# MLP of a two-layer diffusion step: the residual's tiles pass one by one to the up matrix's rings, and the down matrix's first piece gets a buffer of its own

## The chip, the cores and the metric

The kernel runs on one core of a Trainium2 chip. The metric is the device time of one launch in microseconds (us); lower is better. PE is the matmul engine (TensorE), DVE, ACT and POOL are VectorE, ScalarE and GpSimd, SP is the engine that issues most DMA transfers.

## The reference, cut to what matters

One inference step of a two-layer backbone: layer 0 mixes tokens with an RG-LRU, layer 1 with latent attention, and each layer ends in an MLP with a squared ReLU. All of it is fp32. There are 1024 latent tokens and 128 context tokens, of width 1024; the hidden width is 4096.

```python
def sq_relu_mlp(h, w1, w2):
    a = jax.nn.relu(h @ w1)
    return (a * a) @ w2
...
    for l in range(DEPTH):
        sh1, sc1, g1, sh2, sc2, g2 = adaln_params(c, ada_w[l], ada_b[l])
        h = modulate(rms_norm(xs, norm_mix[l]), sh1, sc1)
        ...  # token mixer -> out
        xs = xs + g1[:, None, :] * out
        h = modulate(rms_norm(xs, norm_mlp[l]), sh2, sc2)
        xs = xs + g2[:, None, :] * sq_relu_mlp(h, mlp_w1[l], mlp_w2[l])
```

## The kernel before, in words

The 1152 tokens stand as columns, in three chunks of 384. The residual `X` is three SBUF tiles `X[c]` of 128 x 8 x 384 fp32 (12 KB in each partition), in a pool `xp`. An fp32 product is made from three matmuls (`mm3`: L148, L151, L152) of a high and a low part of each operand. A weight piece is 128 x 1024: a load on SP's queue gives `raw` (L112), a cast on ACT gives `whi` (L166), a subtraction on DVE or POOL gives `wlo` (L167). The two results go to slots that `wslot` takes in turn from a list of pools, `wcycle`.

`mlp` runs once for each layer, at some 500 to 1290 us and 2040 to 2800 us of the span. Its up matrix takes chunks 0 and 1 with seven products per 2 x 2 block (Strassen-Winograd), and chunk 2 plainly:

- `filler(0, 8)`: the first 8 plain pieces on chunk 2.
- 16 chains `p`, 108 matmuls each. `prep(p + 1, 0..2)`, called at three places within chain `p`, loads two raws (`r`) for the next chain, makes R0 and R1 (splits on POOL in layer 0, on DVE in layer 1), subtracts within the raws (`add`, L459) and splits them again as TY and TX on DVE. Eight hidden results of a chain are squared or summed in tiles `st` and stored to DRAM (`put`, L422: from ACT's queue, or from SP's in `tail`). The pool `upx` holds 8 `st` tiles, 4 `raw` tiles and one `whi`/`wlo` pair (the slot "u" of `wcycle`), in the place of `xp`, which is released before the chains: the residual lies in DRAM (`xs_d`) meanwhile. In layer 0 two jobs `ada` stand in each chain: a load of a row block of the conditioning matrix (L181) and two dot products on DVE (L172).
- `filler(8, 8, bring)`: the last 8 plain pieces on chunk 2, 24 matmuls each. `upx` is released and `xp` allocated anew. After each piece `bring` issues a load of half an X tile (L586, 768 KB) and some loads of hidden halves (`load`, L570, 384 KB, each with a cast on ACT and a subtraction on DVE).

The down matrix follows: `prep_down` makes its pieces V[0], V[1], ... two from each raw. An even V is split from the raw as it came; then four subtractions change the raw (L607) and the odd V is split from it, all of this on POOL. The splits go first to four slots "g" of the pool `gx`, which takes the place of chunk 2's high and low parts (`gpool`). Every third "g" slot first does one `ada` job, in a buffer of `gx` with the tag "ada". The first products use V[0], V[2], then V[1]; each result is added to X by DVE (`residual`, L339).

A scheduler reorders the instructions on each engine, by its own model of times. Only what `keep_in_program_order` marks keeps its place. Tiles of a released pool are taken over one at a time, when the last reader of what lay there is done.

Of the kernel before, what the change touches and what calls it, by code (L numbers as in the profile page):

```python
# [15 lines left out]
D = 1024  # L16
# [4 lines left out]
CH = 384  # L21
NCH = 3
# [43 lines left out]
class Emit:  # L66
    def __init__(self, nc, tc, ins, outs):
        self.nc, self.tc, self.I, self.O = nc, tc, ins, outs
        self.piece_i = 0
        self.opened = []  # L70
        self.pending = []
        self.wpx = None
        self.pin = False
        self.cap = 1 << 30
        self.upx = self.gx = None
        self.on_dve = False
        self.wcycle, self.wi = ["wp"], 0
        self.ready = []
        self.used, self.oldest = set(), 0
        self.ada_i = 0  # L80
        self.ada_jobs = []
        self.ada_quota = 0.0
        self.ada_rate = 0.0
# [31 lines left out]
    def wslot(self):  # L115

        kind = self.wcycle[self.wi % len(self.wcycle)]
        self.wi += 1
        if kind == "g":
            if self.ada_i % 3 == 0:  # L120
                self.ada(1, self.gx)
            self.ada_i += 1
        pool, n = {"wp": (self.wp, 3), "x": (self.wpx, 1), "u": (self.upx, 1), "g": (self.gx, 4)}[kind]
        return tuple(pool.tile([128, 1024], F32R, tag=t, name=t, bufs=n) for t in ("whi", "wlo"))

    def wsplit(self, raw, eng, n=1024):
# [287 lines left out]
    def mlp(self, p0, base, l, H, after_acc, after):  # L414
        nc = self.nc
        hid_d = self.hid_d[l]

        up_row = lambda m: base + (m // 4) * 8 + m % 4
# [29 lines left out]
        filler(0, 8)  # L448
        for c in range(NCH):
            self.need(c)  # L450
        self.release(self.xp)
        self.upx = self.alloc(name="upx", bufs=1, side="right", reuse_waits="tile")
        st = lambda: self.upx.tile([128, CH], F32, tag="st", name="st", bufs=8)
        A11, A12 = (tuple(t[:, 4 * i:4 * i + 4] for t in H[0]) for i in range(2))
        A22 = tuple(t[:, 4:8] for t in H[1])
        C2 = [tuple(t[:, 4 * i:4 * i + 4] for t in H[2]) for i in range(2)]
# [5 lines left out]
        def prep(p, part):  # L462
            if p == 16:
                if part:
                    self.on_dve = True
                    self.cap = p0 + 8 + part
                    self.prefetch(self.cap)
                return
            m = 4 * (p // 2) + p % 2
            if part == 0:  # L470
                r = [self.raw(up_row(i), *((self.upx, 4) if p else ())) for i in (m, m + 2)]
                W[p] = {"r": r, "R0": self.wsplit(r[0], leng)}
                return
            w = W[p]
            r0, r1 = w["r"]
            a, b = slice(0, 512), slice(512, 1024)
            if part == 1:
                w["R1"] = self.wsplit(r1[:, b], leng, 512)
                add(r0[:, a], r1[:, a], r0[:, a], ALU.subtract)
                add(r1[:, a], r1[:, b], r1[:, a], ALU.subtract)  # L480
                add(r1[:, b], r1[:, b], r0[:, a], ALU.subtract)
                add(r0[:, b], r0[:, b], r1[:, b], ALU.subtract)
            else:
                w["TY"] = self.wsplit(r1, nc.vector)
                w["TX"] = self.wsplit(r0, nc.vector)

        self.wcycle, self.wi = ["wp", "wp", "wp", "x", "u"], 0
        for i in range(3):
            prep(0, i)
        tail = None  # L490
        for p in range(16):
            m = 4 * (p // 2) + p % 2
            w = W.pop(p)
            if p == 15:
                self.wcycle, self.wi = ["wp", "wp", "wp", "x"], 0
            A = self.bank()
            self.prod(A, w["R0"], 0, A11, 4, True)
# [1 line left out]
            nc.scalar.copy(out=s1, in_=A)  # L499
            if tail:  # L500
                tail()
            prep(p + 1, 0)
            B = self.bank()
            self.prod(B, w["R0"], 4, A12, 4, True)
# [29 lines left out]
            square(h12)  # L534
            put(m, 0, h12)
            prep(p + 1, 2)

            def tail(m=m, A=A, w=w, h11=h11, h12=h12, h22=h22):
                self.prod(A, w["TX"], 4, A22, 4)
                h21, s, d = st(), st(), st()  # L540
                relu2(h21, A)
                add(s, h21, h22)
                put(m, 4, s, nc.sync)
                add(h21, h11, h21, ALU.subtract)
                put(m, 6, h21, nc.sync)
                add(d, s, h11, ALU.subtract)
                put(m, 3, d, nc.sync)
                e = st()
                add(e, h12, d, ALU.subtract)
                put(m, 7, e, nc.sync)  # L550
# [2 lines left out]
                self.ada(2, pin=True)  # L553
        tail()
        self.cap = p0 + 16
        self.release(self.upx)
        self.xp = self.alloc(name="xp", bufs=3, side="right", reuse_waits="tile")
        self.X = []
        D = {}
        used = [0]  # L560

        def load(upto, pin=False):
            while used[0] < min(upto, 72):
                i = used[0]
                if i % 2 == 0:
                    D["t"] = self.cbig(F32R, "hid")
                t = D["t"]
                o = 4 * (i % 2)
                hi, lo = t[:, o:o + 2], t[:, o + 2:o + 4]
                ld = nc.sync.dma_start(lo.bitcast(F32), hid_d[i // 9][:, i % 9])  # L570
                if pin:
                    self.tc.keep_in_program_order(ld)
                self.split(hi, lo, lo.bitcast(F32))
                D[i] = (hi, lo)
                used[0] += 1

        for c in range(NCH):
            self.X.append(self.xp.tile([128, 8, CH], F32, tag="X", name="X"))
        xh = [(c, i) for c in range(NCH) for i in (0, 4)]

        def bring(i):

            if 2 <= i:
                c, k = xh[i - 2]
                self.tc.keep_in_program_order(
                    nc.sync.dma_start(self.X[c][:, k:k + 4], self.xs_d[l][c, :, k:k + 4])  # L586
                )
            load((2, 4, 5, 6, 7, 8, 9, 9)[i], True)

        filler(8, 8, bring)  # L590
        self.on_dve = False
# [5 lines left out]
        V = []  # L597

        def prep_down(upto):
            while len(V) < min(upto, 64):  # L600
                n = len(V)
                if n % 2 == 0:
                    raw = D["raw"] = self.raw(base + (n // 8) * 8 + 4 + n // 2 % 4)
                else:
                    raw = D["raw"]
                    b11, b21, b12, b22 = (raw[:, i * 256:(i + 1) * 256] for i in range(4))
                    sub = lambda out, x, y: nc.gpsimd.tensor_tensor(out=out, in0=x, in1=y, op=ALU.subtract)  # L607
                    sub(b11, b12, b11)
                    sub(b12, b22, b12)
                    sub(b22, b22, b11)  # L610
                    sub(b21, b21, b22)
                V.append(self.wsplit(raw, nc.gpsimd))

        def add_x(c, m, ps):
            self.residual(c, m, ps, l, 5)
# [2 lines left out]
        for d in range(16):  # L618
            g = d // 2
            a12, a11, ca, s2, s1, cb, s3, s4, a22 = (D[9 * g + i] for i in range(9))  # L620
            ch = []
            for i in range(2):
                n = 2 * d + i
# [951 lines left out]
```

## Time and profile before

| | us |
|---|---|
| median of 3 runs (lowest, highest) | 2833.51 (2833.25, 2837.84) |
| profiled execution | 2835.06 |
| its span, from the first to the last instruction | 2833.2 |
| PE busy | 2656.6 (94%) |
| DVE, ACT, POOL busy | 1951.3, 1385.0, 840.8 |
| mean granted PE clock | 0.974 |

A row of the page's costliest groups has line, engine, operation, output<-inputs, shape and count, then the busy time and the mean in ns, then the idle time of the engine just before, with what ended it. In a timeline each row has start and duration in us; the brackets give the idle time before it and its releaser. A `q` behind an engine's name (SPq, ACTq) is that engine's queue issuing a DMA; the row's duration is that of the issue, not of the transfer.

### The profile page before, as it was taken

What the parts mean: (1) busy time and instruction counts of PE and PEld (TensorE: products, weight loads), DVE (VectorE), ACT (ScalarE), POOL (GpSimd) and SP (SyncE); (2) the same over time, 40 slices, a digit from 0 to 9 for tenths busy, and PEclk for the clock granted to TensorE, in tenths of its full rate; (3) what the DMA queues carried; (4) which work ended last, traced back from release to release, by engine and by line L of the source; (5) the groups of instructions that cost most, each with busy time, mean ns of one, the idle gap of its engine ahead of it and who ended that gap; (6) DMA issues with size and microseconds to landing.
All of it is one profiled execution on the core that took longest, in us unless ns stands there. A gap on an engine that the chain in (4) does not pass through costs nothing. (4 is left out here: it accounts for less than half of the span.)

```text
span 2833.2 us, 40867 instructions
## 1 busy us (share of the span) xinstructions
PE 2656.6 (94%) x15355; PEld 2561.3 (90%) x15355; DVE 1951.3 (69%) x3461; ACT 1385.0 (49%) x2446; POOL 840.8 (30%) x544
## 2 busy tenths in 40 slices
PE   5999999999996899997998999998999999799997
PEld 2878798999996899997987999998999999799997
DVE  7778876788865987779455767761675554477777
ACT  3577843645453232334325878881465544333332
POOL 1000013221214877771341000001300000677774
PEclk9999999999997999999998999999999999899998
DMA  6122244455556443434244111116344445433333
GB/s 255 45 82 82 82 156 139 142 189 185 199 176 235 158 136 112 134 101 158 68 132 141 62 48 62 35 52 220 115 153 138 134 144 194 150 123 113 122 124 107
DMA packets 145718, 368.67 MB, mean 130 GB/s; under 512 B 15472, under 2 KB 77744, under 8 KB 143088
## 3 DMA queue, kind: packets, MB, share of 16 engines
q1 hardware_dynamic: 121712, 331.44, 34.7%
q10 hardware_dynamic: 23040, 31.47, 3.1%
q0 software_dynamic: 768, 3.15, 0.4%
q8 instruction: 121, 1.98, 0.3%
q14 instruction: 77, 0.63, 0.1%
HBM read 268.83 MB, written 94.54 MB: 128 GB/s over the span
## 5 line engine op out<-in xcount | busy, mean ns | idle before, releaser
L167 POOL TENSOR_TENSOR wlo<-raw,whi 128x1024 fp32r<-128x1024 f32 x217 | 526.5, 2436 | 1680.8 <-ACT whi L166 1066.1
L166 ACT CAST whi<-raw 128x1024 fp32r<-128x1024 f32 (+1 forms) x349 | 347.2, 1009 | 637.3 <-POOL raw L607 261.1
L148 PE MATMUL ps<-hhi,whi 128*128 128x384 f32 x1576 | 533.0, 342 | 28.5 <-ACT hhi L324 13.2
L151 PE MATMUL ps<-hlo,whi 128*128 128x384 f32 x1576 | 535.3, 340 | 16.3 <-DVE hlo L325 16.1
L152 PE MATMUL ps<-hhi,wlo 128*128 128x384 f32 x1576 | 530.6, 339 | 1.2 <-DVE wlo L167 1.2
L339 DVE SCALAR_TENSOR_TENSOR X<-ps,mod,X 128x384 f32<-128x384 f32 (+2 forms) x768 | 380.4, 534 | 218.7 <-PE ps L152 186.2
L148 PE MATMUL ps<-hid,whi 128*128 128x384 f32 x1408 | 477.2, 342 | 38.8 <-ACT whi L166 20.5
L151 PE MATMUL ps<-hid,whi 128*128 128x384 f32 x1408 | 477.8, 339 | 0.0
L152 PE MATMUL ps<-hid,wlo 128*128 128x384 f32 x1408 | 463.3, 339 | 2.1 <-POOL wlo L167 2.1
L148 PEld LDWEIGHTS ps<-hhi,whi 128*128 128x128 f32 x1576 | 299.1, 190 | 38.7 <-ACT hhi L324 14.4
L151 PEld LDWEIGHTS ps<-hlo,whi 128*128 128x128 f32 x1576 | 300.0, 190 | 21.1 <-DVE hlo L325 21.0
L148 PEld LDWEIGHTS ps<-hid,whi 128*128 128x128 f32 x1408 | 268.8, 191 | 49.9 <-ACT whi L166 23.4
L152 PEld LDWEIGHTS ps<-hhi,wlo 128*128 128x128 f32 x1576 | 299.3, 190 | 3.5 <-DVE wlo L167 2.6
L152 PEld LDWEIGHTS ps<-hid,wlo 128*128 128x128 f32 x1408 | 267.3, 191 | 3.3 <-POOL wlo L167 3.3
L151 PEld LDWEIGHTS ps<-hid,whi 128*128 128x128 f32 x1408 | 269.4, 191 | 0.0
L167 DVE TENSOR_TENSOR wlo<-raw,whi 128x1024 fp32r<-128x1024 f32 (+1 forms) x132 | 151.6, 1158 | 164.8 <-ACT whi L166 163.8
L167 DVE TENSOR_TENSOR hid<-hid 128x768 fp32r<-128x768 f32 x144 | 204.2, 1440 | 77.0 <-ACT hid L166 77.0
L607 POOL TENSOR_TENSOR raw<-raw 128x256 f32<-128x256 f32 x256 | 244.4, 958 | 17.6
L166 ACT CAST hid<-hid 128x768 fp32r<-128x768 f32 x144 | 117.1, 834 | 138.1 <-DMA hid<-hid 119.1
L1277 DVE TENSOR_REDUCE mx<-ps 128x1 f32<-128x384 f32 (+1 forms) x200 | 108.6, 543 | 76.0 <-PE ps L1276 74.5
L151 PE MATMUL ps<-S,whi 128*128 128x384 f32 x384 | 129.2, 336 | 2.7 <-DVE S L167 2.7
L152 PE MATMUL ps<-S,wlo 128*128 128x384 f32 x384 | 129.0, 336 | 0.0
(213 smaller groups left out, 5190.0 us busy)
## 6 DMA issues: line engine op xcount, KB each, us to landing
raw<-wts SPq DMA_DIRECT2D x221, 512.0 KB, 3.7
hid<-hid SPq DMA_DIRECT2D x144, 384.0 KB, 4.3
raw<-ada_wt SPq DMA_DIRECT2D x56, 512.0 KB, 5.4
hid<-st ACTq DMA_DIRECT2D x128, 192.0 KB, 2.0
hid<-st SPq DMA_DIRECT2D x128, 192.0 KB, 2.0
adaw<-ada_n SPq DMA_DIRECT2D x24, 512.0 KB, 4.4
xs<-X SPq DMA_DIRECT2D x6, 1536.0 KB, 5.3
X<-xs SPq DMA_DIRECT2D x12, 768.0 KB, 10.7
```

The source lines that it names most:

```text
L148: mm = nc.tensor.matmul(ps, lhsT=w[0], rhs=h[0], start=first, stop=False, **kw)
L151: nc.tensor.matmul(ps, lhsT=w[0], rhs=h[1], start=False, stop=False, **kw)
L152: nc.tensor.matmul(ps, lhsT=w[1], rhs=h[0], start=False, stop=last, **kw)
L166: nc.scalar.copy(out=hi, in_=src)
L167: (lo_eng or nc.vector).tensor_tensor(out=lo, in0=src, in1=hi.bitcast(F32), op=ALU.subtract)
L339: self.nc.vector.scalar_tensor_tensor(out=self.X[c][:, m, a:b], in0=ps[:, a:b], scalar=self.mod[:, l, j, cond, m:m + 1], in1=self.X[c][:, ...
L607: sub = lambda out, x, y: nc.gpsimd.tensor_tensor(out=out, in0=x, in1=y, op=ALU.subtract)
L1277: nc.vector.tensor_reduce(out=mx[:, j:j + 1], in_=ps, axis=AX.X, op=ALU.max)
```

## The change

Three edits, in both layers.

Rings. `xp` is not released. Of its three tiles of 12 KB one becomes a ring of 8 `st` tiles, one a ring of 3 `raws` tiles (4 `raw` tiles before), and the third is `u`, allocated anew for each use. The very first chain's raws come from the common buffers, as before.

X. With no pool to release, chunks 0 and 1 come back during the last chain (`bring_x`, four half loads), once the rings that lay there are read out; only chunk 2's two halves are left to the plain pieces (i = 5, 6). The slot "u" leaves `wcycle` one chain earlier (p == 14).

Down matrix. V[0]'s raw has a buffer of its own: the "ada" buffer of `gx`. V[0] and V[1] are made on DVE, the rest on POOL. The `ada` jobs come at every third "g" slot still, but at the last of three and not at the first; one job fewer falls into the down matrix, and one more behind it.

```diff
-            if self.ada_i % 3 == 0:
+            if self.ada_i % 3 == 2:
...
+        if kind == "u":
+            t = self.xp.tile([128, 8, CH], F32R, tag="X", name="u").rearrange("p a b -> p (a b)")
+            return t[:, :1024], t[:, 1024:2048]
...
-        self.release(self.xp)
-        self.upx = self.alloc(name="upx", bufs=1, side="right", reuse_waits="tile")
-        st = lambda: self.upx.tile([128, CH], F32, tag="st", name="st", bufs=8)
+        big = lambda name, dt=F32: self.xp.tile([128, 8, CH], dt, tag="X", name=name)
+        st_t, raw_t = big("st"), big("raws").rearrange("p a b -> p (a b)")
+        ring = {"st": 0, "raw": 0}
...
+        def up_raw(i):
+            ring["raw"] += 1
+            o = ring["raw"] % 3 * 1024
+            nc.sync.dma_start(raw_t[:, o:o + 1024], self.I["wts"][up_row(i)])
+            return raw_t[:, o:o + 1024]
...
-                r = [self.raw(up_row(i), *((self.upx, 4) if p else ())) for i in (m, m + 2)]
+                r = [up_raw(i) if p else self.raw(up_row(i)) for i in (m, m + 2)]
...
+        def bring_x(c, k):
+            self.tc.keep_in_program_order(nc.sync.dma_start(self.X[c][:, k:k + 4], self.xs_d[l][c, :, k:k + 4]))
...
-            if p == 15:
+            if p == 14:
                 self.wcycle, self.wi = ["wp", "wp", "wp", "x"], 0
...
+            if p == 15:
+                self.X = [big("X") for _ in range(2)]
+                bring_x(0, 0)
+                bring_x(0, 4)
             prep(p + 1, 0)
...
-            if 2 <= i:
-                c, k = xh[i - 2]
-                self.tc.keep_in_program_order(
-                    nc.sync.dma_start(self.X[c][:, k:k + 4], self.xs_d[l][c, :, k:k + 4])
-                )
-            load((2, 4, 5, 6, 7, 8, 9, 9)[i], True)
+            if i in (5, 6):
+                bring_x(2, 4 * (i - 5))
+            load((2, 4, 5, 6, 7, 8, 8, 9)[i], True)
...
+                eng = nc.vector if n < 2 else nc.gpsimd
                 if n % 2 == 0:
-                    raw = D["raw"] = self.raw(base + (n // 8) * 8 + 4 + n // 2 % 4)
+                    row = base + (n // 8) * 8 + 4 + n // 2 % 4
+                    if n == 0:
+                        raw = self.gx.tile([128, 1024], F32, tag="ada", name="raw", bufs=1)
+                        nc.sync.dma_start(raw, self.I["wts"][row])
+                    else:
+                        raw = self.raw(row)
+                    D["raw"] = raw
...
-                V.append(self.wsplit(raw, nc.gpsimd))
+                V.append(self.wsplit(raw, eng))
```

Three places in the order of the instructions follow; a row has the line, the operation, output<-input, the shape, and how many stand in a row. The line numbers of the changed kernel are a little larger: L465 is the load of a ring's raw, L507 that of X, L594 that of a hidden half, L624 that of V[0]'s raw, L184 ada's, L425 `put`, L170 the low part, L631 the four subtractions.

SP, layer 0, from the last stores of the last chains on (`hid_7` and `hid_0` are blocks of the hidden tensor in DRAM), before:

```order
L422 DMA hid_7<-st 128x384 x4
L112 DMA raw<-wts 128x1024 x2
L570 DMA hid<-hid_0 128x768 x4
L586 DMA X<-xs 128x1536
L570 DMA hid<-hid_0 128x768
L112 DMA raw<-wts 128x1024
L586 DMA X<-xs 128x1536
L570 DMA hid<-hid_0 128x768
L112 DMA raw<-wts 128x1024
L586 DMA X<-xs 128x1536
```

and now (the first row is chain 14's stores, the stores of chain 15 are the fifth and seventh rows):

```order
L425 DMA hid_7<-st 128x384 x4
L507 DMA X<-xs 128x1536 x4
L184 DMA raw<-ada_wt 128x1024 x2
L112 DMA raw<-wts 128x1024
L425 DMA hid_7<-st 128x384 x3
L112 DMA raw<-wts 128x1024
L425 DMA hid_7<-st 128x384
L594 DMA hid<-hid_0 128x768 x2
L112 DMA raw<-wts 128x1024
L594 DMA hid<-hid_0 128x768 x2
```

Four of the X loads have moved ahead of chain 15's stores and of all hidden loads; they stood between the hidden loads and the raws of the plain pieces.

SP, layer 0, a little later, where the plain pieces end and the down matrix begins, before:

```order
L586 DMA X<-xs 128x1536
L570 DMA hid<-hid_0 128x768
L586 DMA X<-xs 128x1536
L570 DMA hid<-hid_1 128x768 x3
L112 DMA raw<-wts 128x1024 x2
L181 DMA raw<-ada_wt 128x1024 x2
L112 DMA raw<-wts 128x1024
```

and now:

```order
L507 DMA X<-xs 128x1536
L594 DMA hid<-hid_0 128x768
L507 DMA X<-xs 128x1536
L594 DMA hid<-hid_0 128x768
L594 DMA hid<-hid_1 128x768 x3
L112 DMA raw<-wts 128x1024 x2
L624 DMA raw<-wts 128x1024
L184 DMA raw<-ada_wt 128x1024
L112 DMA raw<-wts 128x1024
```

V[0]'s raw, one of the two at L112 before, is now L624, behind the two raws of V[2] and V[4]; it waits for the last matmul of the plain pieces, the last reader of what lay in its buffer.

POOL, layer 0, at the start of the down matrix, before and then now:

```order
L167 TENSOR_TENSOR wlo<-raw,whi 128x1024
L607 TENSOR_TENSOR raw<-raw 128x256 x4
L167 TENSOR_TENSOR wlo<-raw,whi 128x1024 x2
L607 TENSOR_TENSOR raw<-raw 128x256 x2
L167 TENSOR_TENSOR wlo<-raw,whi 128x1024
```

```order
L170 TENSOR_TENSOR wlo<-raw,whi 128x1024
L631 TENSOR_TENSOR raw<-raw 128x256 x4
L170 TENSOR_TENSOR wlo<-raw,whi 128x1024 x2
L631 TENSOR_TENSOR raw<-raw 128x256 x4
L170 TENSOR_TENSOR wlo<-raw,whi 128x1024 x2
```

The rows read alike, but the first piece was V[0] and is V[4] now. V[0] and V[1] are on DVE, behind the hidden halves' low parts:

```order
L170 TENSOR_TENSOR hid<-hid 128x768 x6
L170 TENSOR_TENSOR wlo<-raw,whi 128x1024
L631 TENSOR_TENSOR raw<-raw 128x256 x4
L342 SCALAR_TENSOR_TENSOR X<-ps,mod,X 128x384 x2
L170 TENSOR_TENSOR wlo<-raw,whi 128x1024
```

The same six instructions have moved from POOL to DVE in layer 1.

More of the change, by code (lines that the diff above doesn't have):

```diff
@@ L74, in __init__ @@
         self.cap = 1 << 30
-        self.upx = self.gx = None
+        self.gx = None
         self.on_dve = False
@@ L119, in wslot @@
         if kind == "g":
-            if self.ada_i % 3 == 0:
+            if self.ada_i % 3 == 2:
                 self.ada(1, self.gx)
             self.ada_i += 1
-        pool, n = {"wp": (self.wp, 3), "x": (self.wpx, 1), "u": (self.upx, 1), "g": (self.gx, 4)}[kind]
+        if kind == "u":
+            t = self.xp.tile([128, 8, CH], F32R, tag="X", name="u").rearrange("p a b -> p (a b)")
+            return t[:, :1024], t[:, 1024:2048]
+        pool, n = {"wp": (self.wp, 3), "x": (self.wpx, 1), "g": (self.gx, 4)}[kind]
         return tuple(pool.tile([128, 1024], F32R, tag=t, name=t, bufs=n) for t in ("whi", "wlo"))
@@ L450, in mlp, with st @@
             self.need(c)
-        self.release(self.xp)
-        self.upx = self.alloc(name="upx", bufs=1, side="right", reuse_waits="tile")
-        st = lambda: self.upx.tile([128, CH], F32, tag="st", name="st", bufs=8)
+        big = lambda name, dt=F32: self.xp.tile([128, 8, CH], dt, tag="X", name=name)
+        st_t, raw_t = big("st"), big("raws").rearrange("p a b -> p (a b)")
+        ring = {"st": 0, "raw": 0}
+        def st():
+            ring["st"] += 1
+            return st_t[:, ring["st"] % 8]
+        def up_raw(i):
[3 more added lines that the diff above has]
+            return raw_t[:, o:o + 1024]
         A11, A12 = (tuple(t[:, 4 * i:4 * i + 4] for t in H[0]) for i in range(2))
@@ L523, in mlp @@
             prep(p + 1, 1)
+            if p == 15:
+                bring_x(1, 0)
             self.prod(A, w["TY"], 0, S3, 4)
@@ L536, in mlp @@
             prep(p + 1, 2)
+            if p == 15:
+                bring_x(1, 4)
             def tail(m=m, A=A, w=w, h11=h11, h12=h12, h22=h22):
@@ L555, in mlp @@
         self.cap = p0 + 16
-        self.release(self.upx)
-        self.xp = self.alloc(name="xp", bufs=3, side="right", reuse_waits="tile")
-        self.X = []
+        self.X.append(big("X"))
         D = {}
@@ L575, in load @@
                 used[0] += 1
-        for c in range(NCH):
-            self.X.append(self.xp.tile([128, 8, CH], F32, tag="X", name="X"))
-        xh = [(c, i) for c in range(NCH) for i in (0, 4)]
         def bring(i):
-            if 2 <= i:
-                c, k = xh[i - 2]
-                self.tc.keep_in_program_order(
-                    nc.sync.dma_start(self.X[c][:, k:k + 4], self.xs_d[l][c, :, k:k + 4])
-                )
-            load((2, 4, 5, 6, 7, 8, 9, 9)[i], True)
+            if i in (5, 6):
+                bring_x(2, 4 * (i - 5))
+            load((2, 4, 5, 6, 7, 8, 8, 9)[i], True)
         filler(8, 8, bring)
@@ L606, in prep_down @@
                     b11, b21, b12, b22 = (raw[:, i * 256:(i + 1) * 256] for i in range(4))
-                    sub = lambda out, x, y: nc.gpsimd.tensor_tensor(out=out, in0=x, in1=y, op=ALU.subtract)
+                    sub = lambda out, x, y: eng.tensor_tensor(out=out, in0=x, in1=y, op=ALU.subtract)
                     sub(b11, b12, b11)
```

## The prediction

> **What bounds the kernel now.** I read the busy shares first, then TensorE (PE) by stretches of time around the places that the diff touches, then the rows of PE in which it sat idle, and from each of these back to what released it. PE is busy for 94% of the span, so the question is where the rest is lost.
>
> The stretches have these columns: length, busy time (and count) of PE, its weight loads, DVE, ACT and POOL, the granted clock, the DMA share and GB/s.
>
> ```profile
> 600.00:843.00 243.00, 242.61 (x1385) 241.14 (x1384) 187.93 (x268) 122.06 (x219) 43.17 (x23) 1.00 0.53 183
> 843.00:909.00 66.00, 42.12 (x196) 38.87 (x197) 33.32 (x36) 24.95 (x35) 20.03 (x13) 0.79 0.71 263
> 909.00:1000.00 91.00, 82.71 (x433) 80.21 (x432) 82.55 (x126) 25.71 (x28) 79.13 (x48) 0.93 0.46 151
> ...
> 2100.00:2411.00 311.00, 311.00 (x1783) 311.00 (x1782) 163.18 (x235) 159.86 (x275) 0.00 (x0) 1.00 0.47 157
> 2411.00:2444.00 33.00, 17.58 (x74) 15.48 (x74) 13.29 (x19) 12.98 (x18) 17.75 (x16) 0.69 0.42 158
> ```
>
> In the chains of both layers PE has no room: 1783 matmuls in 311 us, 0.174 us each, at clock 1.00. In layer 0, 843 to 909 us (chunk 2's last plain columns, then the start of the down matrix) holds 196 matmuls, 34.2 us of work at that rate, in 66 us: 31.8 us too many. In layer 1, 2411 to 2444 us holds 74, 12.9 us, in 33: 20.1 too many. These two holes are what this change can reach. Cut finer:
>
> ```profile
> 843.00:861.00 18.00, 17.12 (x96) 16.47 (x96) 8.37 (x8) 8.94 (x13) 0.00 (x0) 1.00 0.98 360
> 861.00:873.60 12.60, 0.00 (x0) 0.00 (x0) 0.93 (x1) 2.81 (x5) 0.00 (x0) 0.62 1.02 415
> 873.60:878.00 4.40, 4.11 (x12) 3.60 (x13) 3.45 (x5) 3.97 (x6) 0.00 (x0) 0.54 1.01 403
> 878.00:884.50 6.50, 6.50 (x37) 6.19 (x36) 3.58 (x5) 3.51 (x6) 0.00 (x0) 1.00 0.63 245
> 884.50:908.00 23.50, 13.43 (x49) 11.64 (x48) 15.99 (x18) 5.73 (x7) 19.03 (x12) 0.71 0.32 98
> ...
> 2423.50:2434.30 10.80, 8.57 (x24) 7.12 (x25) 1.28 (x3) 2.90 (x5) 9.25 (x7) 0.51 0.12 26
> 2434.30:2444.00 9.70, 8.31 (x48) 7.99 (x47) 5.02 (x9) 2.10 (x2) 8.49 (x10) 1.00 0.12 47
> ```
>
> The DMA engines are full (share 0.98 to 1.02) exactly where PE stops in layer 0. The rows of PE that end an idle time, with its length and releaser in brackets:
>
> ```profile
> 873.64 0.69 PE L148 MATMUL ps<-hhi,whi 128*128 128x384 f32 x1 [12.88 <-ACT whi L166]
> ...
> 887.32 0.44 PE L148 MATMUL ps<-hid,whi 128*128 128x384 f32 x1 [2.80 <-ACT whi L166]
> ...
> 889.75 0.69 PE L152 MATMUL ps<-hid,wlo 128*128 128x384 f32 x1 [1.28 <-POOL wlo L167]
> ...
> 895.77 0.69 PE L148 MATMUL ps<-hid,whi 128*128 128x384 f32 x1 [3.09 <-ACT whi L166]
> ...
> 908.04 0.45 PE L148 MATMUL ps<-hid,whi 128*128 128x384 f32 x1 [2.93 <-DVE X L339]
> ```
> ```profile
> 2423.56 0.69 PE L148 MATMUL ps<-hid,whi 128*128 128x384 f32 x1 [11.86 <-ACT whi L166]
> ...
> 2425.99 0.69 PE L152 MATMUL ps<-hid,wlo 128*128 128x384 f32 x1 [0.79 <-POOL wlo L167]
> ...
> 2430.30 0.69 PE L148 MATMUL ps<-hid,whi 128*128 128x384 f32 x1 [1.38 <-ACT whi L166]
> ...
> 2443.25 0.45 PE L148 MATMUL ps<-hid,whi 128*128 128x384 f32 x1 [1.39 <-ACT whi L166]
> ```
>
> Who held ACT back: in layer 0 ACT's queue stood before a store of a hidden tile (issued 871.44) until an X load had landed, and the cast of a weight piece stood behind it. In layer 1 V0's raw was issued at 2411.49 and cast only at 2422.46.
>
> ```profile
> 871.44 0.33 ACTq L422 DMA_DIRECT2D hid<-acc  x1
> 871.81 0.83 ACT L166 CAST hid<-hid 128x768 fp32r<-128x768 f32 x1 [8.30 <-DMA X<-xs]
> 872.55 1.04 ACT L166 CAST whi<-raw 128x1024 fp32r<-128x1024 f32 x1
> ```
> ```profile
> 2411.49 2.41 SPq L112 DMA_DIRECT2D raw<-wts  x2
> ```
> ```profile
> 2422.46 1.04 ACT L166 CAST whi<-raw 128x1024 fp32r<-128x1024 f32 x1
> ```
>
> The price of a load in the jam (847 to 884 us) and out of it (2444 to 2520 us); columns count, size, median us to landing:
>
> ```profile
> X<-xs SPq DMA_DIRECT2D x6, 768.0 KB, 10.5
> raw<-wts SPq DMA_DIRECT2D x5, 512.0 KB, 7.3
> ```
> ```profile
> raw<-wts SPq DMA_DIRECT2D x9, 512.0 KB, 3.6
> ```
>
> **The change, part by part.**
>
> **X[0] and X[1] in the last chain.** Four of the six X loads (4 x 768 KB) leave the jam and are issued behind chain 14's stores, a whole chain (108 matmuls of 0.174, 19 us) ahead of the columns, where 600 to 843 us shows the queues at 183 GB/s against 415 in the jam. Only two X loads stay with chunk 2's columns. The store that held ACT's queue waits for no jammed X load then, and the 12.88 us go. Until 884.5 us, 145 matmuls (25.3 us at the full rate) took 41.5 us: 16.2 too many. Of these the idle time is 12.88, the half-rate stretch 873.6 to 878 us 2.3 (12 matmuls, 2.1 us of work, in 4.4), the rest small waits. Late hidden loads or the two X loads left may keep some 0.6 us. I take -15.6 us; the ends are -16.2 and -8 (half of the idle time kept, if the two X loads still hold a store).
>
> In layer 1 the columns had no stall before 2411 us, so the same move gives nothing there directly.
>
> **V0's raw in a buffer of its own, V0 and V1 on DVE.** In the order of SP, V0's load now waits for the last plain matmul of chunk 2, because gx, where its buffer lies, takes the place of chunk 2's hidden tile. So it is issued at that moment and not before: 3.6 us to land (the calm row), 1.04 cast, some 0.4 of issue and semaphores, 5.0 us of idle PE in each layer. That is a new wait, and it stands against 11.86 us in layer 1 and 2.80 in layer 0 (where V0's raw had landed early, since that layer's columns ended late).
>
> Layer 1: idle 11.86 to 5.0, -6.9. The half-rate stretch: 24 matmuls, 4.2 us of work, in 10.8, of which 2.2 are the waits (0.79, 1.38) and 4.4 the clock; after a gap of 5 us I take 3.4 (about what the stretch after 873.6 lost, with a window more), -1.0. The three small waits, 0.79, 1.38 and 1.39, are POOL's: split 2.35, four subs, split, one after the other; with V0 and V1 on DVE, V2 to V5 start at once on POOL, -3.5. Sum -11.4, from 31.5 us (2411.70 to 2443.25) to some 20.
>
> Layer 0: 884.5 to 908 holds 48 matmuls, 8.4 us of work, so 15.1 too many, 10.1 of it idle. After: 5.0 of idle for V0, 3.4 to 5 of half clock, and the wait for V2 and V4, whose loads go out with the ada loads, 3 to 6 us more. That is 12 to 15, so 0 to -3; with the port question below up to +4. I take -0.4.
>
> What DVE pays: two splits at 1.18 and four subs, each half of a 128x512 one of 0.68, together 3.8 us per layer, where DVE is 68% busy (15.99 of 23.5). POOL loses two splits and four subs of the row below, and has no other work ahead of V2.
>
> ```profile
> 704.22 2.36 DVE L167 TENSOR_TENSOR wlo<-raw,whi 128x1024 fp32r<-128x1024 f32 x2 [1.01 <-ACT whi L166]
> ...
> 711.72 0.68 DVE L459 TENSOR_TENSOR raw<-raw 128x512 f32<-128x512 f32 x1
> ```
> ```profile
> 889.78 4.87 POOL L607 TENSOR_TENSOR raw<-raw 128x256 f32<-128x256 f32 x4
> ```
>
> **Rings in the chains.** With three raw slots instead of four, the second raw of the chain after next can be loaded only when TX is split, 706.58 in the rows above; its first reader is the subtraction at 711.72. The load has 5.1 us. Loads there take 4.1 us (weights) and 6.8 (ada):
>
> ```profile
> raw<-wts SPq DMA_DIRECT2D x24, 512.0 KB, 4.1
> raw<-ada_wt SPq DMA_DIRECT2D x22, 512.0 KB, 6.8
> ```
>
> 1.0 us to spare at the median, 1.7 short at the slower figure, and behind that DVE has the 1.01 us of idle of the row at 704.22 to give before TY and TX are late. Taken at 0, with an upper end of 0.5 us for each of layer 0's 15 chains (+7.5); in layer 1 no ada loads compete. The ring for the stores (8 slots as before) and `u` in the third X tile change no count: 0.
>
> **Later in the down matrix.** The waits for X there stay: nothing in the change makes L339 faster. They bound a gain I do not count:
>
> ```profile
> PE ps L148 <- DVE X L339: 8.3, 5, 2.8
> ```
>
> The ada dots come in every third slot still, shifted by two, so the first comes two slots later, and one dot pair goes to the attention part: 0, ends -5 and +3.
>
> **Sum.** -15.6 - 0.4 - 11.4 = -27.4 us on the profiled execution, 2835.06, which gives 2807.7. The median of the runs is 2833.51, 1.55 lower, so 2806.1. About 0.2%, 5.7 us, is what a measurement of this kernel can tell from no change.
>
> **Two rules of the skill weighed.** After 873.64, behind 12.88 us of idle, the matmuls ran at 0.54 of the clock for 4 us; after 2423.56 at 0.51 for 10.8. The Trainium skill ("TensorE: Matmul & The Clock Gate", Part 1, "What's actually happening") says that an idle window of about 3.4 us drops the array to half rate and a busy one of the same length restores it. By that rule the 5.0 us gap that stays still costs a half-rate stretch, which is what the sum has; were the gap under 3.4, both layers would gain some 3 us more.
>
> The second speaks against the change. A dot on DVE took 3.28 us at 895.97, while POOL was splitting, and 1.23 at 906.22:
>
> ```profile
> 895.97 3.28 DVE L172 SCALAR_TENSOR_TENSOR junk<-raw,cb 128x1024 bf16<-128x1024 f32 x1 [2.24 <-DMA raw<-ada_wt]
> ...
> 906.22 1.23 DVE L172 SCALAR_TENSOR_TENSOR junk<-raw,cb 128x1024 bf16<-128x1024 f32 x1 [2.98 <-DMA raw<-ada_wt]
> ```
>
> So work of V0 and V1 on DVE beside V4's on POOL may run one at a time: a split 1.18 to 3.3, each sub 0.34 to some 1.2, at worst 2 x 2.1 + 4 x 0.9 = 7.8 us per layer, of which V0's split (2.1) lies on the path at once and the rest behind the 24 matmuls (4.2 us) of V0 and V2. That is 2 to 6 us per layer. The Trainium skill ("SBUF — State Buffer", "Who interferes with whom") calls this pair of ports an exclusive lock between a DVE instruction with two SBUF inputs and GpSimd; the trace agrees in direction, 3.28 against 1.23.
>
> **The rivals.**
>
> Jam stays (0.15). V0's load goes out at the columns' end together with hidden loads, V2's, V4's and ada's. If it takes 7.3 us (the jam's row) and not 3.6, each layer loses 3.7 us, and the half-rate stretch grows by one window (1.7): about +11 in all, 2817. For: two X loads, hidden halves and V2's to V5's raws still go out around that moment. Against: four of the six big loads are gone.
>
> Port lock (0.10). As worked out, 4 to 12 us back, 2814.
>
> Rings stall every chain (0.07), the slower end. If the late raw makes PE wait in each of 30 chains, the whole gain is gone at 27.4/30 = 0.9 us per chain; at 1.3 the time is 2845. For it speaks that the load has 5.1 us and ada's take 6.8; against, that PE idled 0.39 us in the whole of 600 to 843, that DVE has slack and that layer 1 has no ada loads.
>
> Nothing moves (0.05). The hole is bound by the total of loads, 263 GB/s over 843 to 909, and only its place changes; or the last chain stalls by what the columns gain: 2830. Against: the chains' queues run at 183 GB/s.
>
> More than the sum (0.03). The X waits (8.3) and their half clock go as well, since the down matrix starts with POOL ahead: 2793.
>
> My forecast, with 0.60, has its own range from 2798 to 2814.
>
> **How the numbers follow.** Faster by over 0.2%: 0.60 + 0.15 + 0.10 + 0.03 = 0.88; within: 0.05; slower: 0.07. The range 2793 to 2822 reaches from the case of more to the jam's (2817, with its half of 5 us on top) and leaves out the stalls and the unmoved hole, 0.12, and a little of the rest.
>
> **What would show it.** Right: the 12.88 us of idle in layer 0 gone, the columns of both layers ending without a stall; a single idle time of some 5 us for `whi` of V0 behind a load issued at the last plain matmul; X loads of chunks 0 and 1 in the last chain; chains at clock 1.00. Wrong: idle rows in the chains released by the subtractions on `raws`; V0's load landing over 6 us after its issue; DVE's splits of V0 and V1 at 3 us; a stall of chunk 2's columns behind a store or the last two X loads.

## The result, and the profile after

The changed kernel takes 2817.78 us (median of 4 runs, 2816.72 to 2818.61) against 2833.81 of the kernel before beside it: ratio 0.9934, 95% interval 0.9923 to 0.9946. That is 16.0 us less; 27.4 were forecast. The time lies outside the forecast's own range (2798 to 2814) and inside the wide one (2793 to 2822). The profiled execution has a span of 2815.7 us, 17.5 below the one before. One of the ten executions of experiment 2 took 5908.7 us and is left out of its ratio.

PE executes its matmuls in nearly the same order in both kernels, so the same point of the program can be found in both traces. The difference in its time (after minus before) shows where the time went:

| point in the program | before, us | after, us | difference |
|---|---|---|---|
| layer 0, first of the last 8 plain pieces | 834.5 | 830.5 | -4.0 |
| layer 0, last plain matmul | 884.5 | 868.1 | -16.4 |
| layer 0, first matmul of the down matrix (V0) | 887.3 | 877.3 | -10.0 |
| 48 matmuls later | 908.0 | 894.7 | -13.4 |
| 200 matmuls after V0 | 936.6 | 929.7 | -7.0 |
| end of layer 0's down matrix | 1288.2 | 1279.9 | -8.3 |
| layer 1, last plain matmul | 2411.7 | 2405.7 | -6.0 |
| layer 1, V0 | 2423.6 | 2410.6 | -12.9 |
| 66 matmuls later | 2443.3 | 2428.0 | -15.3 |
| end of layer 1's down matrix | 2810.9 | 2793.4 | -17.5 |

The same stretches as before, of the changed kernel (length, busy time and count of PE, weight loads, DVE, ACT, POOL, granted clock, DMA share, GB/s):

```profile
600.00:830.00 230.00, 230.00 (x1320) 230.00 (x1319) 180.06 (x254) 117.14 (x209) 44.59 (x23) 1.00 0.57 201
830.00:868.00 38.00, 35.16 (x196) 33.60 (x194) 20.43 (x25) 18.80 (x29) 0.00 (x0) 1.00 0.91 317
868.00:877.30 9.30, 0.08 (x1) 0.00 (x0) 4.61 (x5) 7.33 (x11) 1.76 (x1) 0.65 0.71 282
877.30:895.00 17.70, 12.82 (x49) 11.17 (x50) 13.14 (x16) 4.98 (x5) 15.91 (x12) 0.79 0.22 67
895.00:1010.00 115.00, 103.13 (x546) 99.75 (x545) 106.33 (x155) 31.30 (x35) 87.99 (x53) 0.94 0.46 153
```

The plain columns (second row) run at clock 1.00, 196 matmuls in 38 us. What is left of the hole lies in the third row: PE stands while DMA moves 282 GB/s. And in the last row DVE is busy for 92% and PE's clock is 0.94. PE's rows at these places, and ACT's and SP's rows that explain the first two:

```profile
877.32 0.69 PE L151 MATMUL ps<-hid,whi 128*128 128x384 f32 x1 [9.24 <-ACT whi L169]
...
923.16 0.69 PE L151 MATMUL ps<-hid,whi 128*128 128x384 f32 x1 [4.08 <-DVE X L342]
...
2410.64 0.69 PE L151 MATMUL ps<-hid,whi 128*128 128x384 f32 x1 [4.97 <-ACT whi L169]
```
```profile
868.11 0.33 SPq L624 DMA_DIRECT2D raw<-wts  x1
...
2405.70 0.33 SPq L624 DMA_DIRECT2D raw<-wts  x1
```
```profile
876.22 1.05 ACT L169 CAST whi<-raw 128x1024 fp32r<-128x1024 f32 x1 [0.81 <-DMA raw<-wts]
...
2409.54 1.05 ACT L169 CAST whi<-raw 128x1024 fp32r<-128x1024 f32 x1 [1.29 <-DMA raw<-wts]
```

V0's load goes out at the last plain matmul in both layers, as the order of the instructions said. In layer 1 it is cast 3.84 us later, in layer 0 only 8.11 us later. SP's rows just before show what went out ahead of it: X's last two loads and six hidden halves from 855 us on, and V2's and V4's raws from 863.93. When V0's load was issued, both X loads had landed (the later at 867.11 us), but three hidden halves and both raws were still under way. The last line is of the three raws from 863.9 us on, V2's, V4's and V0's, with the median from issue to landing:

```profile
857.22 0.43 SPq L507 DMA_DIRECT2D X<-xs  x1
857.75 4.47 SPq L594 DMA_DIRECT2D hid<-hid  x4
863.93 1.74 SPq L112 DMA_DIRECT2D raw<-wts  x2
868.11 0.33 SPq L624 DMA_DIRECT2D raw<-wts  x1
```
```profile
raw<-wts SPq DMA_DIRECT2D x3, 512.0 KB, 8.6
```

### The profile page after: what moved, and what is told of

Same layout as the page of the kernel before. It is cut to its first block, busy times and chain, and to the rows that moved or that the text cites. A ratio compares the mean times of both kernels' runs of the same rounds, so it can differ in the third digit from the quotient of the medians.

```text
span 2815.7 us, 40793 instructions
## 1 busy us (share of the span) xinstructions
PE 2651.3 (94%) x15355; PEld 2559.8 (91%) x15355; DVE 1955.2 (69%) x3473; ACT 1385.9 (49%) x2446; POOL 833.2 (30%) x532
## 5 line engine op out<-in xcount | busy, mean ns | idle before, releaser
L170 POOL TENSOR_TENSOR wlo<-raw,whi 128x1024 fp32r<-128x1024 f32 x183 | 459.1, 2520 | 1445.9 <-ACT whi L169 1201.0
L342 DVE SCALAR_TENSOR_TENSOR X<-ps,mod,X 128x384 f32<-128x384 f32 (+2 forms) x768 | 379.5, 535 | 202.8 <-PE ps L155 169.3
L154 PE MATMUL ps<-hlo,whi 128*128 128x384 f32 x1432 | 486.2, 340 | 15.2 <-DVE hlo L328 15.0
L169 ACT CAST whi<-raw 128x1024 fp32r<-128x1024 f32 x229 | 235.6, 1046 | 538.0 <-POOL raw L631 238.6
L151 PE MATMUL ps<-hhi,whi 128*128 128x384 f32 x1432 | 483.1, 341 | 15.5 <-ACT hhi L327 14.1
L155 PE MATMUL ps<-hhi,wlo 128*128 128x384 f32 x1432 | 483.9, 339 | 2.5 <-DVE wlo L170 2.5
L151 PEld LDWEIGHTS ps<-hhi,whi 128*128 128x128 f32 x1432 | 271.9, 190 | 24.3 <-ACT hhi L327 15.6
L154 PEld LDWEIGHTS ps<-hlo,whi 128*128 128x128 f32 x1432 | 272.7, 190 | 19.0 <-DVE hlo L328 19.0
L631 POOL TENSOR_TENSOR raw<-raw 128x256 f32<-128x256 f32 x248 | 239.7, 966 | 19.1
L170 DVE TENSOR_TENSOR hid<-hid 128x768 fp32r<-128x768 f32 x144 | 201.0, 1417 | 55.7 <-ACT hid L169 55.6
L170 DVE TENSOR_TENSOR wlo<-raws,whi 128x1024 fp32r<-128x1024 f32 (+1 forms) x72 | 81.0, 1135 | 96.2 <-ACT whi L169 95.4
L1316 ACT ACTIVATE p<-ps,nm 128x384 f32<-128x384 f32 (+1 forms) x200 | 113.0, 579 | 28.6 <-DVE nm L1311 28.0
L169 ACT CAST whi<-raws 128x1024 fp32r<-128x1024 f32 (+1 forms) x96 | 89.3, 939 | 58.3 <-PE ps L154 44.1
```

What stands on the lines that cost most here:

```text
L151: mm = nc.tensor.matmul(ps, lhsT=w[0], rhs=h[0], start=first, stop=False, **kw)
L154: nc.tensor.matmul(ps, lhsT=w[0], rhs=h[1], start=False, stop=False, **kw)
L155: nc.tensor.matmul(ps, lhsT=w[1], rhs=h[0], start=False, stop=last, **kw)
L169: nc.scalar.copy(out=hi, in_=src)
L170: (lo_eng or nc.vector).tensor_tensor(out=lo, in0=src, in1=hi.bitcast(F32), op=ALU.subtract)
L342: self.nc.vector.scalar_tensor_tensor(out=self.X[c][:, m, a:b], in0=ps[:, a:b], scalar=self.mod[:, l, j, cond, m:m + 1], in1=self.X[c][:, ...
```

## The experiments

Each was measured beside the kernel before on one chip, and the chips differ, so ratios are compared and not times. Diffs are against the changed kernel unless the text says otherwise.

**1. Rings and X alone.** V0 as in the kernel before:

```diff
-            if self.ada_i % 3 == 2:
+            if self.ada_i % 3 == 0:
...
-                eng = nc.vector if n < 2 else nc.gpsimd
+                eng = nc.gpsimd
...
-                    if n == 0:
-                        raw = self.gx.tile([128, 1024], F32, tag="ada", name="raw", bufs=1)
-                        nc.sync.dma_start(raw, self.I["wts"][row])
-                    else:
-                        raw = self.raw(row)
+                    raw = self.raw(row)
```

> Rings and X loads in the last chain are kept; V0 is as in the kernel before (raw in the common buffers, V0 and V1 on POOL, first ada job at the first of three slots). Theory A (the X loads stalled chunk 2's columns; V0's own buffer pays in layer 1 only): layer 0's columns end at some 868 us without the 12.88 us stall, V0's raw goes out some 4 us before the last column matmul and not after it, so the idle time there is 5 to 6 us instead of 9.24; layer 1's is 4 to 7. Time 2811 to 2820. Rival B (the gain is V0's: its buffer and DVE): 2826 or more. Rival C (the two parts need each other): near 2833.

Measured: 2814.84 us, ratio 0.9926 [0.9911, 0.9940]. This part alone gives all of the gain. The two idle times before V0 are 6.92 us (layer 0; 5 to 6 expected) and 1.14 us (layer 1; 4 to 7 expected, too much).

**2. V0's part alone.** The kernel before, with only the down matrix's edits of the change.

> The kernel before with only the down matrix's part: V0's raw in the ada buffer, V0 and V1 on DVE, ada at the last of three slots. Theory A: the 12.88 us stall of layer 0 stays, since six X loads stay in the columns; V0's idle time there is 5.0 (the jam is over at 884 us); in layer 1 V0's load goes out at the last column matmul as it does before, into the jam, so 8 to 11 us instead of 11.86. Time 2826 to 2836. Rival B: 2816 to 2822, as the changed kernel.

Measured: 2840.22 us, ratio 1.0014 [1.0004, 1.0023]: a little slower. The columns' stall stays (12.83 us). In layer 0 V0 waits 4.98 us, as expected where the jam is over; in layer 1 PE waits 15.76 us, more than the 8 to 11 expected and more than the 11.86 before. The load did not go out at the last plain matmul, as expected, but 6.9 us after its end, behind V2's and V4's raws on SP:

```profile
2419.32 2.44 SPq L112 DMA_DIRECT2D raw<-wts  x2
2425.56 0.33 SPq L607 DMA_DIRECT2D raw<-wts  x1
```

**3. V0's raw in the common buffers, still on DVE.**

```diff
-                    if n == 0:
-                        raw = self.gx.tile([128, 1024], F32, tag="ada", name="raw", bufs=1)
-                        nc.sync.dma_start(raw, self.I["wts"][row])
-                    else:
-                        raw = self.raw(row)
+                    raw = self.raw(row)
```

> The changed kernel with V0's raw in the common buffers again, V0 and V1 still on DVE. V0's load then waits only for the split of column piece 14, not for the last column matmul. Theory A1 (layer 0's 9.24 us is the late issue): V0 is issued some 4 us earlier, idle time 5 to 6; V4's raw is late instead. Time 2812 to 2817. Theory A2 (it is the amount of data ahead of it, two X loads, four hidden halves and two raws at 420 GB/s): V0 lands hardly earlier, 7 to 9 us of idle, 2817 to 2820.

Measured: 2806.98 us, ratio 0.9897 [0.9882, 0.9912], outside the changed kernel's interval and below both expectations. PE's first matmul of the down matrix, in layer 0 and in layer 1:

```profile
874.96 0.69 PE L151 MATMUL ps<-hid,whi 128*128 128x384 f32 x1 [5.40 <-ACT whi L169]
```
```profile
2399.74 0.45 PE L151 MATMUL ps<-hid,whi 128*128 128x384 f32 x1 [1.14 <-ACT whi L169]
```

9.24 and 4.97 us have become 5.40 and 1.14: 3.8 us less in each layer. In layer 1 the clock stays up as well (1.00 over the next 15 us, 0.76 over 13 in the changed kernel):

```profile
2399.70:2415.00 15.30, 13.36 (x71) 12.19 (x72) 10.23 (x17) 5.00 (x6) 9.79 (x9) 1.00 0.16 48
```
```profile
2410.60:2424.00 13.40, 10.97 (x44) 10.14 (x45) 8.50 (x12) 2.94 (x3) 10.54 (x10) 0.76 0.05 9
```

So V0's own buffer costs 0.0037 of 2834, some 10 us; A1 was right on the wait and too low on its price. From the last plain matmul to 48 matmuls of the down matrix (66 in layer 1) this kernel is 7.4 and 6.8 us faster than the changed one. That is more than the 3.8 us, since in layer 0 the waits behind V0 shrink too, and in layer 1 the half clock is gone.

**4. The X loads back among the columns**, i = 2 to 7; rings and V0's part stay.

```diff
-            if i in (5, 6):
-                bring_x(2, 4 * (i - 5))
-            load((2, 4, 5, 6, 7, 8, 8, 9)[i], True)
+            if i >= 2:
+                bring_x((i - 2) // 2, 4 * (i % 2))
+            load((2, 4, 5, 6, 7, 8, 9, 9)[i], True)
```

and no `bring_x` in chain 15.

> The changed kernel with all six X loads back among chunk 2's columns (i = 2 to 7, hidden halves as in the kernel before); rings and V0's part stay. Theory A: the stall of 10 to 13 us in layer 0's columns is back, V0's idle time there is 5 to 7; layer 1's V0 waits 8 to 11 us. What the chains gained (3.9 us in layer 0 before 790 us) stays. Time 2824 to 2833. Rival B (rings or V0 carry the gain): 2817 to 2821.

Measured: 2834.33 us, ratio 0.9993 [0.9983, 1.0002]. The place of the X loads is worth 0.0059, some 17 us. But the mechanism was met only in part: layer 0's columns stall for 3.37 us and not 10 to 13, and it is layer 1 that now stalls, where the kernel before did not. V0's idle time was missed as well, 7.59 us in layer 0 (5 to 7 expected) and 5.15 in layer 1 (8 to 11 expected). The columns of layer 1 and ACT's wait there:

```profile
2413.97 0.69 PE L151 MATMUL ps<-hhi,whi 128*128 128x384 f32 x1 [7.61 <-ACT whi L169]
```
```profile
2409.59 0.33 ACTq L425 DMA_DIRECT2D hid<-acc  x1
2409.96 0.83 ACT L169 CAST hid<-hid 128x768 fp32r<-128x768 f32 x1 [8.62 <-DMA hid<-hid]
```

It is the same kind of wait (a store in ACT's queue that is issued only when an earlier load has landed, here a hidden half, with weight casts behind it). Why it met layer 0 in the kernel before and layer 1 here was not tested.

**5. The ada job at the first of three slots again**, on experiment 3 (`% 3 == 0`).

> As the run with V0's raw in the common buffers (ratio 0.9897), with the ada job at the first of three slots again. Theory A: the dots at the last of three slots fall between the additions to X while POOL is splitting (3.48 and 2.85 us each in the changed kernel) and PE waits 14.2 us for X between 880 and 1020 us of layer 0; with the kernel before's place layer 0 loses nothing there, as in the run without V0's part: 3 to 5 us less, ratio 0.988. Rival B: the place of the dots is indifferent, V0's head start on DVE only moves the X waits (PE is ahead of DVE whatever the order): ratio 0.9890 to 0.9905.

Measured: 2803.80 us, ratio 0.9894 [0.9879, 0.9909], the same as experiment 3, as rival B said. PE's waits for X from 880 to 1270 us are 15.8 us here and 15.5 there.

**6. No ada job in the down matrix**, on experiment 3: three in each of layer 0's chains 2 to 14, the rest ahead of the attention.

```diff
-            if self.ada_i % 3 == 2:
+            if False:
...
-            if p > 1:
-                self.ada(2, pin=True)
+            if 1 < p < 15:
+                self.ada(3, pin=True)
```

> V0's raw in the common buffers; no ada job in the down matrix; three jobs and not two in each of layer 0's chains 2 to 14, none in chain 15; the few left run ahead of the attention. Theory A (the X waits of layer 0's down matrix come from the dots): the 14.2 us of waits for X fall below 4, some 10 to 14 us with their half clock; the chains hold 2.5 us more of DVE work in 18.8 us, which DVE at 77% bears, so they stall 0 to 5 us in all. Ratio 0.985 to 0.988. Rival B (the waits come from POOL's subtractions and splits or from DVE's additions themselves): the waits stay over 8 us and the ratio is 0.989 to 0.993. Rival C: the chains stall on DVE by over 1 us each, ratio 0.992 or more.

Measured: 2803.35 us, ratio 0.9889 [0.9874, 0.9903], the same as experiment 3 again, but by two large opposite terms. From 880 to 1270 us PE waits for X, in experiment 3 and then here:

```profile
PE ps L151 <- DVE X L342: 15.5, 11, 2.9
```
```profile
PE ps L151 <- DVE X L342: 4.7, 5, 2.3
```

Between the last plain matmul and 800 matmuls of the down matrix it gains 20 us on the kernel before (+2.9 to -17.0), where experiment 3 gains nothing (-15.0 to -14.6). In the chains it loses 15.2 us on the kernel before (-0.6 at 500 us to +14.6), where experiment 3 gains 2.3: PE, busy without a gap in the changed kernel, waits 11.5 us for DVE there, in 11 pieces.

```profile
560.00:830.00 270.00, 256.88 (x1445) 251.24 (x1444) 231.60 (x332) 125.03 (x224) 54.93 (x27) 1.00 0.60 202
```
```profile
560.00:830.00 270.00, 270.00 (x1549) 270.00 (x1548) 208.75 (x296) 137.55 (x245) 53.02 (x27) 1.00 0.57 199
```

The first row is this experiment's, DVE 86% busy; the second is the changed kernel's, 77%. Rival C's price (over 1 us a chain) and theory A's gain both came true.

**7. No ada job in chain 15**, on experiment 5, two more in chains 13 and 14.

> As e5_ada_first, with the two ada jobs of chain 15 moved to chains 13 and 14 (three each). Theory A: the idle time at the first column piece after the chains (2.61 and 0.65 us in the run with the common buffers) comes from raw loads that stand behind the ada loads, and these behind the X loads on SP; it goes, 2.5 to 5 us less than e5_ada_first. Rival B: it comes from the X loads filling the queues (768 KB each): the idle time stays, no change.

Measured: 2806.83 us, ratio 0.9902 [0.9887, 0.9916]: no gain. The idle time at the first plain piece went, as theory A said, but PE then stood 3.09 us at a later one (859.27). From the first of these pieces to the last matmul the columns gain 10.7 us on the kernel before; in experiment 5 it is 11.4.

**8. Chunk 2's X loads behind V2's raw**, on experiment 5.

> As e5_ada_first, with chunk 2's two X loads issued behind the raws of V0 and V2 and not at columns 5 and 6. Theory A2 (V0 in layer 0 waits for the data ahead of it in the queues): 1.5 MB less ahead of V0 at 420 GB/s is 3.7 us; the idle time of 5.4 us falls to 2 or less and PE keeps its clock: 3 to 7 us less than e5_ada_first. Rival B: the first additions to X[2] wait for the late load and PE loses the same there: no change or slower.

Measured: 2807.21 us, ratio 0.9912 [0.9895, 0.9929]. V0's idle time in layer 0 fell from 5.65 to 2.26 us, about as A2 said (2 or less):

```profile
870.17 0.44 PE L151 MATMUL ps<-hid,whi 128*128 128x384 f32 x1 [2.26 <-ACT whi L169]
```

V0's raw is issued 8.77 us ahead of the last plain matmul's end (4.98 us in experiment 5), and it lands 9.57 us after its issue (8.62 us there). So without X's loads in front of it, it goes out earlier; it does not land faster. The time came out as rival B said, but not in the place it named. Counted from the last plain matmul, layer 0 keeps its gain: it is ahead of experiment 5 by 3.1 us at 48 matmuls and by 3.6 at 800. Against that stand 2.0 us that experiment 5 is ahead when these columns begin and 2.5 us that this kernel loses at layer 1's V0.

**9 to 11. The dots spread over the whole down matrix**, by keeping their loads and the hidden loads in program order: on experiment 5, on experiment 5 with late X loads, and on the changed kernel alone.

```diff
-                self.ada(1, self.gx)
+                self.ada(1, self.gx, pin=True)
...
-                load(9 * (g + 1) + 12)
+                load(9 * (g + 1) + 12, True)
...
-                load(9 * g + 12 + 2)
+                load(9 * g + 12 + 2, True)
```

> As e5_ada_first (ratio 0.9894), with the ada loads of the down matrix kept in program order with the hidden loads, so that the eleven dot pairs spread over the whole down matrix (some 870 to 1260 us) and do not run one behind the other until 1010 us. Theory A (PE's waits for X in layer 0 come from dots crowded into the first 130 us, while POOL's subtractions lengthen them): the waits for X from 880 to 1020 us fall from some 14 us to 3 to 6, the rest of the down matrix bears a dot pair each 35 us with DVE at 75%: 8 to 14 us less, ratio 0.985 to 0.987. Rival B (each dot pair costs PE a wait wherever it stands, since POOL splits all the time and DVE's additions are always just in time): the same number of waits further on, ratio 0.988 to 0.991.

> As e9_ada_spread, with chunk 2's X loads behind the raws of V0 and V2. Theory A: in the run with late X loads and crowded dots, V0's idle time fell from 5.65 to 2.26 us but PE lost the same at the waits for X; with the dots spread the gain stays, 2 to 5 us less than e9_ada_spread. Rival B: the additions to X[2] wait for the load itself: same as e9_ada_spread or slower.

> The changed kernel (ratio 0.9934) with that edit alone: ada loads spread over the down matrix; V0's raw stays in its own buffer. Theory A: the idle time of 9 us for V0 in layer 0 and 5 us in layer 1 stays, the waits for X shrink: 6 to 12 us less than the changed kernel, ratio 0.989 to 0.9915. Rival B: 0.992 to 0.995.

Measured: 0.9903 [0.9887, 0.9920], 0.9896 [0.9882, 0.9911] and 0.9939 [0.9924, 0.9953]: nothing gained in any. Experiment 9 stands 27.2 us ahead of the kernel before at 800 matmuls (experiment 5: 18.1) and is back at 19.0 when the down matrix ends. The waits for X moved along with the dots: up to 1020 us they fall to 6.0 us (experiment 5: 13.7), as theory A said, and after it they rise to 5.7 (experiment 5: 2.1). Rival B of experiment 9 has the ratio.

**12. V0 and V1 on POOL**, V0's raw in its own buffer:

```diff
-                eng = nc.vector if n < 2 else nc.gpsimd
+                eng = nc.gpsimd
```

> The changed kernel (ratio 0.9934) with V0 and V1 made on POOL again; V0's raw stays in its own buffer. Theory A (DVE takes two splits and four subtractions off POOL's queue, so V2 to V5 are ready sooner; the lengthened DVE instructions beside POOL cost less than that): PE idles more behind V0 in both layers, for V1 and V2, 3 to 9 us slower than the changed kernel, ratio 0.9945 to 0.9965. Rival B (the shared port makes DVE's work serial with POOL's, and delays the additions to X): 0.9915 to 0.9935.

Measured: 2831.80 us, ratio 0.9987 [0.9977, 0.9997]. DVE for V0 and V1 is worth 0.0053, some 15 us, more than theory A's 3 to 9. POOL's rows in layer 1 show why: it is busy almost without a break, and V0 and V1 share it with V2 to V5.

```profile
2417.05 4.65 POOL L170 TENSOR_TENSOR wlo<-raw,whi 128x1024 fp32r<-128x1024 f32 x2 [354.57 <-ACT whi L169]
2421.66 5.52 POOL L631 TENSOR_TENSOR raw<-raw 128x256 f32<-128x256 f32 x8
2427.66 7.04 POOL L170 TENSOR_TENSOR wlo<-raw,whi 128x1024 fp32r<-128x1024 f32 x3 [0.47 <-ACT whi L169]
```

PE waits 4.79, 3.89 and 3.39 us for V0 and for what follows it; after V0 the changed kernel waits 2.39 us once.

**The whole.** The moved X loads give 0.0059, measured by taking them out of the changed kernel. With them and the rings kept, four of the runs cross the other two choices:

| | V0 and V1 on POOL | V0 and V1 on DVE |
|---|---|---|
| V0's raw in the common buffers | 0.9926 (experiment 1) | 0.9894 (experiment 5) |
| V0's raw in its own buffer | 0.9987 (experiment 12) | 0.9934 (changed kernel) |

The first row has the ada job at the first of three slots and the second at the last, which experiments 3 and 5 show to be the same. So DVE is worth 0.0032 (9 us) where V0 comes from the common buffers and 0.0053 (15 us) where it comes late. V0's own buffer costs 0.0061 (17 us) with POOL and 0.0040 (11 us) with DVE, or 0.0037 against experiment 3. Experiments 3 and 5 leave the buffer out: 0.9897 and 0.9894, the fastest simple versions, some 30 us below the kernel before and 10 below the changed one. Nothing tried on top of them moved the time by more than the intervals.

## Why the prediction was right or wrong

The direction and the wide range were right; the size was 1.7 times too large, and the forecast's own range was missed by 4 us.

**Columns of layer 0: -15.6 forecast, -12.5 measured** (the stretch from -4.0 to -16.4). The stall of 12.88 us is gone and the last plain matmul came at 868.1 us. The mechanism was right for PE, but ACT's queue still stood until an X load had landed, for 4.38 us, where the prediction said that no store would wait for one; no wait of PE followed:

```profile
867.55 0.83 ACT L169 CAST hid<-hid 128x768 fp32r<-128x768 f32 x1 [4.38 <-DMA X<-xs]
```

What is missing are small waits in the columns, for which the prediction left 0.6 us. They are 1.32 and 0.64 us, then 0.27 and 0.61:

```profile
840.35 0.45 PE L151 MATMUL ps<-hhi,whi 128*128 128x384 f32 x1 [1.32 <-ACT whi L169]
```

Their cause was tested once: without ada jobs in chain 15 the first of them goes and one further on comes (experiment 7).

**Start of the down matrix in layer 0: -0.4 forecast, +3.0 measured** (-16.4 to -13.4 at 48 matmuls). The step that failed is the price of V0's load, 3.6 us from a calm row, in a place that is not calm: it took 8.11 us to its cast, and the idle time was 9.24 us and not 5.0. The wait for V2 behind it, priced at 3 to 6 us, was 2.66. The rival "Jam stays" had the load right, with 7.3 us from the jam's row, but in layer 0 only. That its total of 2817 lies so near to 2817.78 is luck: half of its price came, and the rest is made up of terms that it did not have. The wait itself, on the last plain matmul, was foreseen; what was not weighed is that the common buffers would have cost less. Experiment 3 shows it, 3.8 us less in each layer, and experiment 8 shows that X's loads ahead on SP hold V0's raw back, another 3.4 us of idle time.

**Later waits for X: 0 forecast, some +5 measured** (-13.4 to -8.3). The term was set to zero because nothing makes L342 (L339 before) faster. That was the wrong test, for the waits can also grow. From 880 to 1270 us, before and after:

```profile
PE ps L148 <- DVE X L339: 12.9, 9, 2.9
```
```profile
PE ps L151 <- DVE X L342: 16.2, 13, 4.1
```

The dots have a part in it: without them the waits are 4.7 us, and the head start grows (experiment 6). Why the waits grow with the change is open. It could be that PE starts earlier and so meets more of DVE's late additions; DVE is 92% busy from 895 to 1010 us (87% before). Experiment 5 fits this (-23.2 at 48 matmuls, -17.6 at the end), and so does experiment 1, with V0 and V1 on POOL (-12.0 and -11.7). Two runs do not fit: experiment 12 also has V0 and V1 on POOL and loses 8.6 us (-9.9 to -1.3), and experiment 2 loses 7.7 with a head start of only 3.2.

**Layer 1: -11.4 forecast, -9.3 measured** to 66 matmuls (-6.0 to -15.3), -11.5 to the end of its down matrix. The idle time of 4.97 us was forecast at 5.0, and two stretches of half clock cost the 3.4 us that the sum had. The term that failed is that of the three small waits, -3.5: one of 2.39 us is there instead. It is a wait for the first additions to X, which stand on DVE behind V1's four subtractions:

```profile
2411.95 3.38 DVE L631 TENSOR_TENSOR raw<-raw 128x256 f32<-128x256 f32 x4
```
```profile
2416.73 0.42 PE L151 MATMUL ps<-hid,whi 128*128 128x384 f32 x1 [2.39 <-DVE X L342]
```

**Chains: 0 forecast, -4.0 in layer 0.** The ring of three raws stalls nothing: from 560 to 830 us PE has no wait at all, and DVE waits 1.3 us for ring loads:

```profile
DVE raws L473 <- DMA raws<-wts: 1.3, 2, 0.7
```

That rival is dead. Part of the gain is a wait of PE for DVE that the kernel before has in that stretch and the changed one has not:

```profile
PE ps L148 <- DVE st L459: 2.2, 3, 1.0
```

Experiments 1 and 4 show the same gain in the chains (from 500 us to the plain pieces, 3.9 and 3.0 us) and experiment 2, without the rings, does not (0.3), so it goes with the rings; how they bring it was not tested. From the end of layer 0 to layer 1's plain pieces 1.1 us were lost, and 1.2 within these; the runs scatter by as much.

**The port.** Its rival took DVE's work to be lengthened by POOL's. It is: four subtractions on DVE took 3.37 us beside POOL's (layer 0, changed kernel) and 1.81 us where POOL stood still (experiment 3):

```profile
879.08 3.37 DVE L631 TENSOR_TENSOR raw<-raw 128x256 f32<-128x256 f32 x4
```
```profile
876.39 1.81 DVE L627 TENSOR_TENSOR raw<-raw 128x256 f32<-128x256 f32 x4
```

The Trainium skill ("SBUF — State Buffer", "Who interferes with whom") names a lock that DVE and GpSimd hold in turn; these two rows agree with it. The two dots that the prediction compares, 3.28 and 1.23 us, do not show POOL's share: POOL was at work beside both, on a split begun at 895.80 us and on subtractions begun at 906.26. As a reason against the edit the rival was wrong: the slow DVE is still 15 us better than POOL's queue (experiment 12), and 9 us better with the common buffers (experiments 1 and 5).

## What to carry to other kernels

When a buffer is chosen for the first piece of a stage, look at what lived there: a buffer that frees only at the previous stage's last instruction turns its load into idle time, here 4 us to the cast in layer 1 and 8 in layer 0, where more loads were under way. Price a load by the traffic at the moment it will be issued, and not by its median elsewhere. A wait is not a constant because nothing makes its engine faster: the waits for X grew from 12.9 to 16.2 us. And spreading that engine's side work only moved the waits here (experiment 9).

## What the runs showed of the hardware that was not expected

A store in ACT's queue that waits for some earlier load holds the weight casts behind it: 8.30 us in layer 0 of the kernel before, 8.62 us in layer 1 of experiment 4.

The clock fell behind shorter gaps than the long ones that the forecast priced. After 1.14 and 1.52 us of idle it stayed at 1.00 (experiment 3, layer 1). After 4.97 us it was 0.76 over the next 13 us, and after 9.24 us 0.79 over the next 18 (rows above). But waits of 2.83 us in the kernel before and of 2.39 (above) and 2.07 us in the changed kernel were enough:

```profile
2492.41 0.69 PE L148 MATMUL ps<-hid,whi 128*128 128x384 f32 x1 [2.83 <-DVE X L339]
```
```profile
894.65 0.69 PE L151 MATMUL ps<-hid,whi 128*128 128x384 f32 x1 [2.07 <-DVE X L342]
```

The stretches of some 3.4 us behind the waits of 2.07 and 2.39 us have a granted clock of 0.51 and 0.50 (third number from the end):

```profile
894.60:898.10 3.50, 3.45 (x11) 3.45 (x12) 2.68 (x4) 0.47 (x1) 3.50 (x2) 0.51 0.39 137
```
```profile
2417.00:2420.40 3.40, 3.40 (x11) 2.99 (x10) 0.71 (x1) 1.31 (x2) 2.96 (x2) 0.50 0.01 2
```

The Trainium skill ("TensorE: Matmul & The Clock Gate", Part 1, "What's actually happening") puts the idle window at about 3.4 us; these waits of 2.07 to 2.83 us do not keep to it.
